# DeltaNet's triangular inverse taken in place in a one-core hybrid layer kernel: the sign moved into the decay products, the negated copy dropped

## The chip, the cores and the metric

The kernel runs on one core of a Trainium2 chip. The metric is the device time of one execution in microseconds. Engines are named as in the profile: PE (TensorE matmul), PEld (its weight load), DVE (VectorE), ACT (ScalarE), POOL (GpSimd), SP (the queue that issues most transfers). On each engine the order of instructions is fixed when the program is built; an instruction whose data are not there holds up all that stand behind it on its engine.

## What is computed

One layer of a hybrid backbone on 128 context and 512 latent tokens, D_MODEL 1024: a token-mixing sub-layer with a gated DeltaNet branch and a short-convolution branch, then a SwiGLU feed-forward part. What the change touches is the DeltaNet's triangular inverse, for 8 heads, 2 directions and chunks of 64 tokens:

```
lower = jnp.where(tri_strict, jnp.einsum('bhncd,bhned->bhnce', kb, k) * decay, 0.0)
tmat = lax.linalg.triangular_solve(eye + lower, jnp.broadcast_to(eye, lower.shape),
                                   left_side=True, lower=True)
u = jnp.einsum('bhnce,bhned->bhncd', tmat, v * beta[..., None])
```

After it a recurrence over the chunks (the scan) makes the outputs and the final state.

## The kernel before, in words

The kernel is written with a tile framework. Instructions are written in program order with priorities; when the program is built, a scheduler orders each engine's instructions by these priorities and by its own estimate of when their data are ready. The order is then fixed. A change in a few instructions of DVE can so move many others, on every engine.

The mixing sub-layer handles the heads in four pairs, 0 to 3. For each pair, `qkv` makes q, k and v by GEMMs, `prepare` makes the chunk matrices, and `scan` runs the recurrence. All GEMMs here are sums of three passes (lines 83, 84, 85), each instruction 128x320; they fill PE in between, in program order at low priority: the GEMMs of `qkv`, `zgate`, `gate_th` and `short`. Of the work around the change:

- `prepare` multiplies the decays `em` and `ea` with the products of k and q from PSUM (L537), copies `em` in quarters into `Md` (L549) and transposes 32x32 blocks on DVE (L553, into `blk`). It negates that into `X` (L554), sets the diagonal to 1 (L555), and takes thirty steps, each of two DVE instructions: `otmp` is a column of `blk` times a row of `X` (L559), and `X` less `otmp` (L561). Two more block transposes give `RT` and `R` (L565, L566).
- PE then makes the off-diagonal blocks: L578 (waits for `RT`), ACT copies `Y` (L583), L589 and L590, and L593 on ACT and L595 on DVE evict them with a factor of -1 into `EW`. L614 and L619/L621 finish `EW`.
- `scan` has eight steps of two halves each: four or eight small matmuls (L643), and then one copy on ACT and one on DVE (L647 or L661) which the next half needs. L673 makes the outputs, L678 to L688 normalise them.
- Interleaved with a pair's inverse, the next pair's `kh` (L448, DVE) is made from a chain of small instructions (L431 to L444), and PE transposes it (L479).
- `row_job` (from the end of pair 3's `prepare` on) adds up modulation rows on DVE, L196, 128x1024 each, from weights of 512 KB.

The tile tag "kb" has one buffer, shared in turn by `kqT`, `blk` and `RT`. The three PSUM buffers of the GEMMs (`d`) are freed by the engine that reads them: for the short convolution these are L716 and L724 on DVE.

Of the kernel before, what the change touches and what calls it, by code (L numbers as in the profile page):

```python
# [9 lines left out]
F32 = mybir.dt.float32  # L10
F32R = mybir.dt.float32r
I32 = mybir.dt.int32
AF = mybir.ActivationFunctionType
ALU = mybir.AluOpType
# [4 lines left out]
P = 128  # L19
# [18 lines left out]
class Kernel:  # L38
# [369 lines left out]
    def prepare(self, p, qkv):  # L408
        nc, dn, dc, g = self.nc, self.da, self.dc, self.g
# [7 lines left out]
        for j in (1, 0, 2):  # L417
            pw = self.psw.tile([P, 1024], F32, name="w", tag="w")
            for t in range(NT):
                nc.tensor.transpose(pw[:, t * P:(t + 1) * P], qkv[j][:, t * P:(t + 1) * P], self.ident)  # L420
            x = dn.tile([P, TOK], F32, name="tk", tag="t25")
            (nc.scalar.copy, nc.scalar.copy, nc.scalar.copy)[j](out=x, in_=pw[:, 0:TOK])
            tok[j] = x
        q, k, v = (tok[j] for j in range(3))
# [31 lines left out]
        for c2 in range(2):  # L456
            s = half(1 - c2)
            for d in range(2):
                nc.gpsimd.tensor_tensor(out=KU[s, d, c2], in1=bc(g["egl"][s, d, :, h2], 64),
                                        in0=self.ident[s, s].unsqueeze(1).unsqueeze(1).broadcast_to([64, NT, 2, 64]),  # L460
                                        op=ALU.mult)
# [14 lines left out]
        for j, x in enumerate((kh, qh)):  # L476
            pw = self.psw.tile([P, 1024], F32, name="w", tag="w")
# [15 lines left out]
        em = dn.tile([P, 2, 2, NT, 64], F32, name="em")  # L493
        ea = dn.tile([P, 2, 2, NT, 64], F32, name="ea")
        for c2 in range(2):
            for t_, d, i in ((em, 0, 0), (em, 1, 2), (ea, 0, 0), (ea, 1, 1)):
                nc.sync.dma_start(out=t_[c2 * 64:c2 * 64 + 64, d].rearrange("p h t x -> p (h t x)"),
                                  in_=g["scr"][i, c2, h2].rearrange("h t x -> (h t x)").unsqueeze(0).broadcast_to([64, TOK]))
# [24 lines left out]
        for ts in (slice(0, 4), slice(4, 5)):  # L523
            m = ts.stop - ts.start
            pw = self.psw.tile([P, 1024], F32, name="w", tag="w")
            for par in range(2):
                for t in range(m):
                    for hd, c2 in ((0, par), (1, 1 - par)):
                        hs = slice(hd * 64, hd * 64 + 64)
                        n = 2 * (ts.start + t) + c2  # L530
                        i = hd * 512 + t * P
                        mm(pw[c2 * 64:c2 * 64 + 64, i:i + P], lhsT=kq3[hs, 0, n, :], rhs=kq3[hs, :, n, :],
                           start=True, stop=True)
            pv = pw.rearrange("p (h t j x) -> p j h t x", h=2, j=2, x=64)[:, :, :, 0:m]
            for e, j in ((em, 0), (ea, 1)):
                for d in range(2):
                    nc.vector.tensor_tensor(out=e[:, d, :, ts], in0=e[:, d, :, ts], in1=pv[:, j], op=ALU.mult)  # L537
        for c2 in range(2):
            nc.gpsimd.dma_start(out=AQ[half(c2), :, c2].rearrange("p d h t x -> p d (h t x)"),
                              in_=ea[half(c2)].rearrange("p d h t x -> p d (h t x)"))  # L540


        Md, EW = self.Md, self.EW
        emv = em.rearrange("p d h t x -> p (d h t) x")
        Ev = [EW[:, :, c2].rearrange("p d h t x -> p d (h t) x") for c2 in range(2)]
        quad = [(c2, b, slice(c2 * 64 + b * 32, c2 * 64 + b * 32 + 32)) for c2 in range(2) for b in range(2)]
        for c2, b, s in quad:
            cp = (nc.vector.tensor_copy, nc.scalar.copy)[b]
            cp(out=Md[s, 0:20], in_=emv[s, :, b * 32:b * 32 + 32])  # L549
        B = dn.tile([P, 32, 32], F32, name="blk", tag="kb")  # L550
        X = dn.tile([P, 32, 32], F32, name="X")
        tmp = dn.tile([P, 256], F32, name="otmp")
        nc.vector.transpose(out=B.rearrange("q r x -> q x r"), in_=Md.rearrange("p m x -> p x m"))  # L553
        nc.vector.tensor_scalar(out=X, in0=B, scalar1=-1.0, scalar2=None, op0=ALU.mult)  # L554
        nc.vector.memset(X.rearrange("q r x -> q (r x)")[:, 0:32 * 32:33], 1.0)  # L555
        for j in range(1, 31):
            n = 31 - j
            t = tmp[:, 0:n * j].rearrange("q (a b) -> q a b", b=j)
            nc.vector.tensor_tensor(out=t, in0=B[:, j + 1:32, j:j + 1].broadcast_to([P, n, j]),  # L559
                                    in1=X[:, j:j + 1, 0:j].broadcast_to([P, n, j]), op=ALU.mult)  # L560
            nc.vector.tensor_tensor(out=X[:, j + 1:32, 0:j], in0=X[:, j + 1:32, 0:j], in1=t, op=ALU.subtract)  # L561

        RT = dn.tile([P, 32, 32], F32, name="RT", tag="kb")
        R = dn.tile([P, 32, 32], F32, name="R")
# [7 lines left out]
        pw = self.psv.tile([P, 1024], F32, name="v", tag="v")  # L572
        Y = dn.tile([P, 20, 32], F32, name="Y")
        for m in range(20):
            for c2 in range(2):
                s0 = slice(c2 * 64, c2 * 64 + 32)
                s1 = slice(c2 * 64 + 32, c2 * 64 + 64)
                mm(pw[s0, m * 32:m * 32 + 32], lhsT=emv[s1, m, 0:32], rhs=RT[s1, m, :], start=True, stop=True,  # L578
                   tile_position=(c2 * 64 + 32, c2 * 64))
        for c2 in range(2):  # L580
            s0 = slice(c2 * 64, c2 * 64 + 32)
            cp = (nc.scalar.copy, nc.scalar.copy)[c2]
            cp(out=Y[s0].rearrange("p m x -> p (m x)"), in_=pw[s0, 0:TOK])  # L583
        pw = self.psv.tile([P, 1024], F32, name="v", tag="v")
# [5 lines left out]
                mm(pw[s1, o], lhsT=Y[s0, 10 + m], rhs=R[s0, 10 + m], start=True, stop=True,  # L590
                   tile_position=(c2 * 64, c2 * 64 + 32))
        for c2, s0, s1 in quads:
            nc.scalar.activation(out=Ev[c2][s0, 0, :, 32:64], in_=pw[s0, 0:320].rearrange("p (m x) -> p m x", x=32),  # L593
                                 func=AF.Copy, scale=-1.0)
            nc.vector.tensor_scalar(out=Ev[c2][s1, 1, :, 0:32], in0=pw[s1, 0:320].rearrange("p (m x) -> p m x", x=32),  # L595
                                    scalar1=-1.0, scalar2=None, op0=ALU.mult)
        return dict(kt=kt, KU=KU, R=RS, AQ=AQ)

    def scan(self, p, pre):
# [139 lines left out]
    def run(self):  # L739
# [422 lines left out]

        def block(ps, A, B, start):
            for k in range(4):
                for n, (x, y) in enumerate(((0, 0), (0, 1), (1, 0))):
                    nc.tensor.matmul(ps, lhsT=A[x][:, k], rhs=B[y][:, k], start=start and k == 0 and n == 0,  # L1166
                                     stop=k == 3 and n == 2, skip_group_check=True)
# [36 lines left out]
        def second(j, v):  # L1204
# [10 lines left out]
            with high():  # L1215
                nc.scalar.copy(out=u2, in_=A)
            B = fd()[:, 0:HALF]
            block(B, o["A12"], B21, True)
# [25 lines left out]
        with tc.manual_schedule(engines={mybir.EngineType.PE}):  # L1244
# [18 lines left out]
            for _ in range(2):  # L1263
                q = quad()
                act += [q[:, i] for i in range(4)]
            prepare(rest[0])
            last = None
            for i, j in enumerate(rest):
                if i + 1 < len(rest):
                    prepare(rest[i + 1], rest[i + 1] < EARLY)  # L1270
                v = first(j)
                if last:
                    third(*last)
                second(j, v)
                last = j, v
# [156 lines left out]
```

## Time and profile before

| | |
|---|---|
| time, median of 3 runs | 1085.77 us (1082.73 to 1088.36) |
| profiled execution: its own time | 1087.67 us |
| profiled execution: its span, first to last instruction | 1085.9 us |
| PE busy | 1021.2 us (94%) |
| DVE busy | 838.9 us (77%) |
| ACT busy | 481.1 us (44%) |

The profiled execution took 1.8 us more than its span, and 1.9 us more than the median of the runs. Pairs 0 to 3 fill the stretch from about 80 us to 460 us of the span; what comes behind are gates, output projections and the feed-forward part.

### The profile page before, as it was taken

Reading aid. Unit: us, or ns where it says so; the run is one execution under the profiler, and the core shown is the slowest. Engines: PE = TensorE matmul, PEld = TensorE weight load, DVE = VectorE, ACT = ScalarE, POOL = GpSimd, SP = SyncE. Lnnn points to the kernel's source line nnn. Section 1 sums busy time; section 2 is a strip of 40 time slices with the busy share of each in tenths; the row PEclk is TensorE's granted clock in tenths of the full one; section 3 lists DMA queues with packets and bytes.
Section 4 is the critical chain, followed back from the end, with each engine's and each line's share of the span. In section 5 each row is a group of like instructions: output and inputs, shape, how many; then the busy total and the mean of one; then the engine's idle time right before and its main releaser. Section 6 shows DMA issues by size and latency. Waiting matters only on the chain.

```text
span 1085.9 us, 19684 instructions
## 1 busy us (share of the span) xinstructions
PE 1021.2 (94%) x7729; PEld 928.0 (85%) x7729; DVE 838.9 (77%) x1702; ACT 481.1 (44%) x923; POOL 142.6 (13%) x168
## 2 busy tenths in 40 slices
PE   6999989988988989999998998999999999999997
PEld 3699988877887888899997888999999999788885
DVE  5767996897898897896896779888787775975336
ACT  5568436415525324425223367444444444623321
POOL 2215421063063060101000000000000000000000
PEclk9999988999999999999999999999999999999999
DMA  9425711254173275555872532323322222552214
GB/s 345 145 91 137 202 54 62 66 127 126 58 174 105 68 165 182 186 180 189 300 234 87 194 126 83 124 96 98 116 79 78 98 78 67 185 172 94 85 39 155
DMA packets 47687, 142.57 MB, mean 131 GB/s; under 512 B 9549, under 2 KB 10066, under 8 KB 47594
## 3 DMA queue, kind: packets, MB, share of 16 engines
q1 hardware_dynamic: 43034, 128.15, 36.2%
q0 software_dynamic: 4560, 13.15, 5.5%
q8 instruction: 61, 1.00, 0.4%
q14 instruction: 32, 0.26, 0.1%
HBM read 118.62 MB, written 12.18 MB: 120 GB/s over the span
## 4 chain that ended last, share of the span: by engine, by line
PE 73%; DVE 16%; ACT 5%; issue 3%; DMA 2%; POOL 1%; SPq 0%; DVEq 0%; ACTq 0%; POOLq 0%
PE acc L1166 19%; PE d L85 8%; PE d L83 8%; PE d L84 8%; PE acc L84 6%; PE acc L83 6%; PE acc L85 6%; PE d L1166 2%; DVE X L561 2%; PE s L643 2%; DVE wl L58 2%; DVE otmp L559 2%; ACT wh L57 1%; PE v L673 1%; PE m L790 1%
## 5 line engine op out<-in xcount | busy, mean ns | idle before, releaser
L83 PE MATMUL d<-hT,wh 128*128 128x320 f32 x720 | 230.0, 320 | 2.0 <-DVE cy L724 2.0
L85 PE MATMUL d<-hT,wl 128*128 128x320 f32 x720 | 230.5, 321 | 0.4 <-DVE wl L58 0.4
L84 PE MATMUL d<-hT,wh 128*128 128x320 f32 x720 | 228.9, 318 | 0.0
L57 ACT CAST wh<-wr 128x512 fp32r<-128x512 f32 x150 | 87.8, 618 | 151.5 <-PE d L84 87.7
L83 PEld LDWEIGHTS d<-hT,wh 128*128 128x128 f32 x720 | 138.9, 193 | 4.6 <-DVE cy L724 2.3
L85 PEld LDWEIGHTS d<-hT,wl 128*128 128x128 f32 x720 | 138.7, 193 | 4.1 <-issue 1.2
L84 PEld LDWEIGHTS d<-hT,wh 128*128 128x128 f32 x720 | 138.8, 193 | 2.2 <-issue 0.5
L58 DVE TENSOR_TENSOR wl<-wr,wh 128x512 fp32r<-128x512 f32 x150 | 102.9, 707 | 40.0 <-ACT wh L57 39.1
L1166 PE MATMUL acc<-mh,wh 128*128 128x320 f32 x288 | 89.6, 311 | 2.0 <-ACT wh L1105 2.0
L1166 PE MATMUL acc<-mh,wl 128*128 128x320 f32 x288 | 89.7, 312 | 0.9 <-DVE wl L1101 0.8
L1166 PE MATMUL acc<-ml,wh 128*128 128x320 f32 x288 | 89.3, 310 | 0.0
L83 PE MATMUL acc<-wh,as 128*128 128x512 f32 x220 | 85.7, 390 | 2.1 <-ACT as L1300 2.1
L84 PE MATMUL acc<-wl,as 128*128 128x512 f32 x220 | 85.6, 389 | 0.0
L85 PE MATMUL acc<-wh,as 128*128 128x512 f32 x220 | 85.5, 389 | 0.0
L196 DVE SCALAR_TENSOR_TENSOR gacc<-wr,cv,gacc 128x1024 f32<-128x1024 f32 x64 | 80.6, 1278 | 4.2 <-DMA wr<-in_w_mod_dram 4.1
L1105 ACT CAST wh<-wr 128x512 fp32r<-128x512 f32 x66 | 40.5, 627 | 72.2 <-PE acc L1166 44.9
L1105 ACT CAST wh<-S 128x512 fp32r<-128x512 f32 x88 | 54.2, 620 | 40.5 <-PE d L1166 17.0
L1101 DVE TENSOR_TENSOR wl<-S,wh 128x512 fp32r<-128x512 f32 x88 | 59.9, 686 | 4.7 <-ACT wh L1105 4.0
L1166 PEld LDWEIGHTS acc<-mh,wh 128*128 128x128 f32 x288 | 54.6, 190 | 2.3 <-ACT wh L1105 2.2
L1166 PEld LDWEIGHTS acc<-mh,wl 128*128 128x128 f32 x288 | 54.5, 189 | 1.4 <-DVE wl L1101 1.4
L1101 DVE TENSOR_TENSOR wl<-wr,wh 128x512 fp32r<-128x512 f32 x66 | 44.8, 688 | 13.9 <-ACT wh L1105 13.2
L1166 PEld LDWEIGHTS acc<-ml,wh 128*128 128x128 f32 x288 | 54.5, 189 | 0.0
(365 smaller groups left out, 2326.2 us busy)
## 6 DMA issues: line engine op xcount, KB each, us to landing
wr<-in_w_ffn_in_dram SPq DMA_DIRECT2D x50, 512.0 KB
wr<-in_w_in_dram SPq DMA_DIRECT2D x45, 512.0 KB
wr<-in_w_mod_dram SPq DMA_DIRECT2D x32, 512.0 KB
wr<-in_w_ffn_out_dram SPq DMA_DIRECT2D x22, 512.0 KB
mr<-in_w_mod_dram SPq DMA_DIRECT2D x16, 512.0 KB
thd<-gt SPq DMA_DIRECT2D x16, 320.0 KB
bth<-thd SPq DMA_DIRECT2D x16, 320.0 KB
wr<-in_w_br_dram SPq DMA_DIRECT2D x8, 512.0 KB
```

The lines of the kernel that those rows point to most:

```text
L57: (high or nc.scalar.copy)(out=hi[:, s], in_=raw[:, s])
L58: (low or nc.vector).tensor_tensor(out=lo[:, s], in0=raw[:, s], in1=hi[:, s].bitcast(F32), op=ALU.subtract)
L83: mm(out, lhsT=ah, rhs=bh, start=start, stop=False)
L84: mm(out, lhsT=ah, rhs=bl, start=False, stop=False)
L85: mm(out, lhsT=al, rhs=bh, start=False, stop=stop)
L196: nc.vector.scalar_tensor_tensor(out=acc[v], in0=w, scalar=self.cv[:, k, v:v + 1], in1=acc[v], op0=ALU.mult, op1=ALU.add)
L559: nc.vector.tensor_tensor(out=t, in0=B[:, j + 1:32, j:j + 1].broadcast_to([P, n, j]), in1=X[:, j:j + 1, 0:j].broadcast_to([P, n, j]), op=A ...
L561: nc.vector.tensor_tensor(out=X[:, j + 1:32, 0:j], in0=X[:, j + 1:32, 0:j], in1=t, op=ALU.subtract)
L643: mm(ps[half(c2), o:o + 64], lhsT=w(d, c2, t, hd), rhs=R[:, d, c2, t, hd, :], start=True, stop=True)
L1101: tt = lambda o, a, b, op: nc.vector.tensor_tensor(out=o, in0=a, in1=b, op=op)
L1105: nc.scalar.copy(out=dst[0], in_=src)
L1166: nc.tensor.matmul(ps, lhsT=A[x][:, k], rhs=B[y][:, k], start=start and k == 0 and n == 0, stop=k == 3 and n == 2, skip_group_check=True)
```

## The change

The product with the decays takes the sign: the two multiplications of `em` become scalar_tensor_tensor with -1, those of `ea` with +1. `em` is negated from there on, so the transposed blocks are what L554 made before: L553 writes `X` itself, L554 and the tile `blk` go, the steps read their column from `X`, and add where they subtracted. The off-diagonal products have the sign in `em` already, so the two evictions copy.

```diff
-            for e, j in ((em, 0), (ea, 1)):
+            for e, j, sign in ((em, 0, -1.0), (ea, 1, 1.0)):
                 for d in range(2):
-                    nc.vector.tensor_tensor(out=e[:, d, :, ts], in0=e[:, d, :, ts], in1=pv[:, j], op=ALU.mult)
+                    nc.vector.scalar_tensor_tensor(out=e[:, d, :, ts], in0=e[:, d, :, ts], scalar=sign, in1=pv[:, j],
+                                                   op0=ALU.mult, op1=ALU.mult)
...
-        B = dn.tile([P, 32, 32], F32, name="blk", tag="kb")
         X = dn.tile([P, 32, 32], F32, name="X")
         tmp = dn.tile([P, 256], F32, name="otmp")
-        nc.vector.transpose(out=B.rearrange("q r x -> q x r"), in_=Md.rearrange("p m x -> p x m"))
-        nc.vector.tensor_scalar(out=X, in0=B, scalar1=-1.0, scalar2=None, op0=ALU.mult)
+        nc.vector.transpose(out=X.rearrange("q r x -> q x r"), in_=Md.rearrange("p m x -> p x m"))
...
-            nc.vector.tensor_tensor(out=t, in0=B[:, j + 1:32, j:j + 1].broadcast_to([P, n, j]),
+            nc.vector.tensor_tensor(out=t, in0=X[:, j + 1:32, j:j + 1].broadcast_to([P, n, j]),
                                     in1=X[:, j:j + 1, 0:j].broadcast_to([P, n, j]), op=ALU.mult)
-            nc.vector.tensor_tensor(out=X[:, j + 1:32, 0:j], in0=X[:, j + 1:32, 0:j], in1=t, op=ALU.subtract)
+            nc.vector.tensor_tensor(out=X[:, j + 1:32, 0:j], in0=X[:, j + 1:32, 0:j], in1=t, op=ALU.add)
...
-            nc.scalar.activation(out=Ev[c2][s0, 0, :, 32:64], in_=pw[s0, 0:320].rearrange("p (m x) -> p m x", x=32),
-                                 func=AF.Copy, scale=-1.0)
-            nc.vector.tensor_scalar(out=Ev[c2][s1, 1, :, 0:32], in0=pw[s1, 0:320].rearrange("p (m x) -> p m x", x=32),
-                                    scalar1=-1.0, scalar2=None, op0=ALU.mult)
+            nc.scalar.copy(out=Ev[c2][s0, 0, :, 32:64], in_=pw[s0, 0:320].rearrange("p (m x) -> p m x", x=32))
+            nc.vector.tensor_copy(out=Ev[c2][s1, 1, :, 0:32], in_=pw[s1, 0:320].rearrange("p (m x) -> p m x", x=32))
```

The order that the scheduler makes changes with it on PE, DVE, ACT and SP; POOL's does not. Three places follow. Lines of the changed kernel stand one or two away from those before: the steps' L559 and L561 are L560 and L562, and behind L595 all are one less (the scan's L643 is L642, its copies L647 and L661 are L646 and L660, L673 is L672).

On DVE, at the start of pair 0's inverse, before:

```order
L549 COPY Md<-em 32x640 x2
L553 STREAM_TRANSPOSE blk<-Md 128x32x32
L554 TENSOR_SCALAR X<-blk 128x1024
L555 MEMSET X 128x32
L559 TENSOR_TENSOR otmp<-blk,X 128x30
L561 TENSOR_TENSOR X<-X,otmp 128x30
L559 TENSOR_TENSOR otmp<-blk,X 128x58
L561 TENSOR_TENSOR X<-X,otmp 128x29x2
L559 TENSOR_TENSOR otmp<-blk,X 128x84
L58 TENSOR_TENSOR wl<-wr,wh 128x512 x2
```

and there of the changed kernel:

```order
L551 COPY Md<-em 32x640 x2
L554 STREAM_TRANSPOSE X<-Md 128x32x32
L555 MEMSET X 128x32
L560 TENSOR_TENSOR otmp<-X 128x30
L562 TENSOR_TENSOR X<-X,otmp 128x30
L560 TENSOR_TENSOR otmp<-X 128x58
L562 TENSOR_TENSOR X<-X,otmp 128x29x2
L560 TENSOR_TENSOR otmp<-X 128x84
L562 TENSOR_TENSOR X<-X,otmp 128x28x3
L560 TENSOR_TENSOR otmp<-X 128x108
L562 TENSOR_TENSOR X<-X,otmp 128x27x4
L58 TENSOR_TENSOR wl<-wr,wh 128x512 x2
```

The negated copy is gone, and the weight split `wl` (L58, for a GEMM) stands three instructions of the inverse further back.

On PE, in the second half of pair 3's scan, before (L83 to L85 are GEMM passes):

```order
L643 MATMUL s<-RS,EW 64x64 x4
L85 MATMUL d<-hT_75,wl 128x320
L83 MATMUL d<-hT_75,wh 128x320
L84 MATMUL d<-hT_76,wh 128x320
L673 MATMUL v<-RS,AQ 64x64
...
L643 MATMUL s<-RS,KU 64x64 x4
L84 MATMUL d<-hT_76,wh 128x320
```

and there of the changed kernel:

```order
L642 MATMUL s<-RS,EW 64x64 x4
L672 MATMUL v<-RS,AQ 64x64
L642 MATMUL s<-RS,KU 64x64 x4
L642 MATMUL s<-RS,EW 64x64 x4
L672 MATMUL v<-RS,AQ 64x64
L642 MATMUL s<-RS,KU 64x64 x4
...
L672 MATMUL v<-RS,AQ 64x64 x16
L642 MATMUL s<-RS,EW 64x64 x4
L208 MATMUL m<-cph,onesr 1x512 x2
```

Before, GEMM passes stand between the halves of the scan's steps; in the changed kernel none stand there in this part. Counted over the whole order of PE, 1604 GEMM passes stood ahead of the first L614 of pair 3 and 1577 do now; between the L643 group whose GEMM count was 1679 (now 1656) and the last L673 group of the scan stood 89, and stand none now.

On DVE, in the same part of the scan, before:

```order
L661 COPY RS<-s 64x128
L196 SCALAR_TENSOR_TENSOR gacc<-wr,cv,gacc 128x1024
L647 COPY RS<-s 64x128
L196 SCALAR_TENSOR_TENSOR gacc<-wr,cv,gacc 128x1024
L58 TENSOR_TENSOR wl<-wr,wh 128x512
L661 COPY RS<-s 64x128
L58 TENSOR_TENSOR wl<-wr,wh 128x512
L196 SCALAR_TENSOR_TENSOR gacc<-wr,cv,gacc 128x1024
L647 COPY RS<-s 64x128
```

and there of the changed kernel, down to the scan's last copy:

```order
L660 COPY RS<-s 64x128
L196 SCALAR_TENSOR_TENSOR gacc<-wr,cv,gacc 128x1024
L646 COPY RS<-s 64x128
L58 TENSOR_TENSOR cpl<-gacc,cph 128x512 x2
L660 COPY RS<-s 64x128
L716 TENSOR_SCALAR cy<-cx,tapsc 128x640
L379 SCALAR_TENSOR_TENSOR cy<-cx,tapsc,cy 128x10x63
L646 COPY RS<-s 64x128
L58 TENSOR_TENSOR cpl<-gacc,cph 128x512 x2
```

Nine scan copies in a row (L646 and L660 in turn) have one L196 between each two and no `wl` any more; what follows them are the rows shown, with `cy` of the short convolution, which stood ahead of the scan before.

## Rows read from the trace of the kernel before

**Rows 1.** The page: busy us of each engine, share of the span, instructions.

```profile
PE 1021.2 (94%) x7729; PEld 928.0 (85%) x7729; DVE 838.9 (77%) x1702; ACT 481.1 (44%) x923; POOL 142.6 (13%) x168
```

**Rows 2.** Stretches: length, then busy us of PE, PEld, DVE, ACT, POOL, clock.

```profile
100.00:150.00 50.00, 42.42 (x297) 40.50 (x296) 47.71 (x113) 21.84 (x35) 23.33 (x23) 0.93 0.51 138
300.00:350.00 50.00, 43.13 (x496) 41.17 (x498) 47.07 (x108) 19.11 (x36) 27.26 (x30) 0.93 0.59 150
418.90:437.90 19.00, 19.00 (x233) 17.11 (x234) 16.63 (x23) 5.57 (x13) 0.00 (x0) 1.00 0.47 149
437.90:459.10 21.20, 21.20 (x209) 17.29 (x209) 17.29 (x27) 8.84 (x23) 1.22 (x2) 1.00 0.66 216
```

**Rows 3.** PE's timeline: start, us, instruction, idle before and its releaser.

```profile
140.79 1.30 PE L479 MATMUL w<-ident,kh 128*128 128x128 f32 x5 [5.40 <-DVE kh L448]
222.31 0.48 PE L479 MATMUL w<-ident,kh 128*128 128x128 f32 x1 [2.62 <-DVE kh L448]
243.10 0.41 PE L83 MATMUL d<-hT,wh 128*128 128x320 f32 x1 [2.00 <-DVE cy L724]
249.54 1.55 PE L578 MATMUL v<-RT,em 32*32 32x32 f32 x80 [1.92 <-DVE RT L565]
324.91 0.76 PE L479 MATMUL w<-ident,kh 128*128 128x128 f32 x5 [2.06 <-DVE kh L448]
335.84 1.54 PE L578 MATMUL v<-RT,em 32*32 32x32 f32 x80 [2.26 <-DVE RT L565]
```

**Rows 4.** Line 554: duration ns minimum, median, maximum.

```profile
L554 DVE TENSOR_SCALAR X<-blk x4: 674/680/695, 121.0 to 369.2; 128x1024 f32<-128x1024 f32 x4
```

**Rows 5.** DVE's timeline: tensor_tensor and scalar_tensor_tensor, one PSUM input each.

```profile
232.96 0.81 DVE L683 TENSOR_TENSOR ob<-ro,v 128x640 f32<-128x640 f32 x1
234.69 0.89 DVE L688 SCALAR_TENSOR_TENSOR zf<-v,onorm,zf 128x640 f32<-128x640 f32 x1
```

**Rows 6.** DVE's timeline around 400 us and 414 us.

```profile
404.47 0.69 DVE L58 TENSOR_TENSOR wl<-wr,wh 128x512 fp32r<-128x512 f32 x1
408.14 0.47 DVE L716 TENSOR_TENSOR cx<-cx,d 128x320 f32<-128x320 f32 x1
416.24 0.55 DVE L717 TENSOR_SCALAR cy<-cx,tapsc 128x640 f32<-128x640 f32 x1
417.33 0.88 DVE L379 SCALAR_TENSOR_TENSOR cy<-cx,tapsc,cy 128x630 f32<-128x630 f32 x1
```

**Rows 7.** DVE's timeline late in pair 3's scan.

```profile
438.24 0.29 DVE L647 COPY RS<-s 64x128 f32<-64x128 f32 x1
...
451.34 0.28 DVE L647 COPY RS<-s 64x128 f32<-64x128 f32 x1
451.55 1.27 DVE L196 SCALAR_TENSOR_TENSOR gacc<-wr,cv,gacc 128x1024 f32<-128x1024 f32 x1
452.92 0.28 DVE L661 COPY RS<-s 64x128 f32<-64x128 f32 x1
...
454.90 1.29 DVE L58 TENSOR_TENSOR cpl<-gacc,cph 128x512 fp32r<-128x512 f32 x2
...
458.41 0.28 DVE L647 COPY RS<-s 64x128 f32<-64x128 f32 x1
```

**Rows 8.** PE's timeline: GEMM passes at full clock.

```profile
128.19 0.31 PE L83 MATMUL d<-hT,wh 128*128 128x320 f32 x1
128.33 0.31 PE L84 MATMUL d<-hT,wh 128*128 128x320 f32 x1
```

**Rows 9.** Stretches around two idle spells of PE, columns as in rows 2.

```profile
130.00:140.00 10.00, 5.39 (x37) 5.12 (x35) 10.00 (x23) 3.57 (x5) 6.72 (x7) 1.00 0.27 90
140.00:150.00 10.00, 9.21 (x45) 9.24 (x46) 9.03 (x17) 1.99 (x4) 3.45 (x2) 0.66 0.25 88
240.00:250.00 10.00, 6.08 (x60) 5.59 (x60) 9.69 (x24) 2.60 (x6) 0.00 (x0) 1.00 0.58 149
250.00:260.00 10.00, 8.61 (x225) 7.79 (x219) 6.20 (x11) 6.67 (x14) 1.20 (x1) 1.00 0.62 188
```

## The prediction

> **What bounds the kernel now.** The page comes first: PE is busy 94% of the span, DVE 77% [rows 1]. So PE's total work is the floor, and the time moves only with the stretches in which PE waits or runs at a lower clock. The table of stretches shows where: between 100 and 150 us PE is busy 42.42 of 50 us while DVE is busy 47.71; between 300 and 350 it is 43.13 against 47.07 [rows 2]. There DVE is the engine that the others wait for. In pair 3's scan it is the other way round: from 418.9 to 459.1 us PE is busy all the time and DVE four fifths of it [rows 2]. PE's timeline then names the waits in the pairs' stretch: PE, which works in order, stands at the transposes of `kh` for 5.40, 2.62 and 2.06 us, at L578 for `RT` 1.92 and 2.26 us, once at a GEMM for `cy` 2.00 us [rows 3]. All are DVE results that come out among the inverse's instructions. They are what a shorter inverse could win. The covered scan is what a new order could lose.
>
> **Part 1, the copy that goes.** L554 takes 0.68 us, four times [rows 4]: 2.7 us of DVE work. It stands in a chain with no other work of its own (transpose, negate, steps), so nothing hides it from `RT`. The memset and the 240 step instructions keep their counts and shapes; adding in place of subtracting, and reading the column from `X`, change neither the number of inputs nor their place in SBUF, so I take them at nothing. No step waits for a new thing: column j of `X` is last written before step j in both versions. The tag "kb" loses a user: L553 need not wait for `kqT` any more, which it never did in the end.
>
> **Part 2, the sign.** 32 multiplications become scalar_tensor_tensor: 16 of 512 columns, 16 of 128, one input from PSUM. The nearest rows are 0.81 us for a tensor_tensor and 0.89 us for a scalar_tensor_tensor, both of 640 columns with a PSUM input [rows 5]. In proportion that is 0.06 us for 512 and 0.02 us for 128, in sum 1.3 us; the bounds are 0 and 32 times 0.08, or 2.6 us. I take 1.3, since the row differs in having its factor in memory and not as a constant, and nothing says which way that goes. The two evictions become copies of the same size; I take them at nothing, bounded by the 0.08 us by which the two instructions differ [rows 5], for each of 16, either way; they lie beside GEMMs on PE. So the direct saving on DVE is 2.7 - 1.3 = 1.4 us, worth 0.1% if all of it reached the end.
>
> **Part 3, the new order ahead of pair 3's scan.** Counting DVE's order between the block transpose L553 and `RT`, each pair loses the 0.68 us copy, and some work moves past `RT`: for pair 0 an L381 with half the columns of the 0.88 us L379 [rows 6], some 0.5 us, for pairs 1 and 2 a scan copy of 0.29 us [rows 7] and an L716 of 0.47 us [rows 6], for pair 3 two `wl` of 0.69 us [rows 6]. That makes about 1.2, 1.0, 1.3 and 2.0 us, 5.5 in sum; less 1.3 for part 2 the chain of inverses comes 4.2 us earlier to pair 3's scan. PE's order answers to it: at its first L614 of pair 3 PE has done 1577 GEMM passes and not 1604. A pass starts every 0.14 to 0.15 us (128.19, 128.33) [rows 8], so 27 passes are 4.0 us of PE work put off till later. 4.2 us earlier with 4.0 us less done is a gain of 0.2 us; I take 0. The bounds: if the moved work only comes back behind `RT`, the chain is 1.4 us earlier and the loss is 2.6 us; if all waits of rows 3 other than the first went, the gain is 2.62 + 2.00 + 1.92 + 2.06 + 2.26 = 10.9 us. I leave the first out because `kh` of pair 1 still stands behind one more step of the inverse, three instructions of 0.4 us, less the copy.
>
> GpSimd shortens what I trust of those waits. The Trainium skill ("SBUF — State Buffer", section "Who interferes with whom") says that a DVE instruction with two SBUF inputs and a GpSimd instruction that reads SBUF lock each other out. By it the inverse's steps keep being caught, as their inputs all stay in SBUF, and the change moves such stalls but removes none; the sum would stand.
>
> **Part 4, pair 3's scan uncovered.** This is the term that decides. Before, 89 GEMM passes stand between the halves of its last steps, and PE is busy for all of the 21.20 us [rows 2]; 89 times 0.147 is 13.1 us, so L643, L673, L208 and L209 have the other 8.1. In the changed order none of the 89 is there. PE must wait after each group of L643 for the copy, and on DVE a 1.27 us L196 stands between each two copies: 451.34 to 452.92 is 1.58 us a half [rows 7]. The nine copies in a row take eight times 1.58 = 12.6 us; then come the `cpl` pair of 1.29 us and a copy of 0.29 [rows 7], and `cy` with 0.55 and 0.88 us [rows 6] and the last copy: 3.3 us. That is 15.9 us between the copies which before lie at 438.24 and 458.41 [rows 7], 20.2 us. So the scan ends 4.3 us sooner, with 13.1 us of GEMMs not done. They come back later, in the stretch from 460 us on where PE has no slack: a loss of 13.1 - 4.3 = 8.8 us. The lower bound is a cadence without L196's full length, say 1.28 us a half, as if a copy could hide: 2.4 us less, 6.4. The upper bound is the old pace: 13.1.
>
> What is queued behind: L673's last group, then the GEMMs. On DVE the short convolution's `cy` (L717 on) now comes at the scan's end, so the second `cy` product and SP's store of it are late by some 20 us, with SP's next weight loads behind that store. Three weights are loaded ahead of the store, though: the GEMM count stands at 1656, and loads up to pass 1824 are ahead of it, 24.7 us of work. I take 0.
>
> **Part 5, the clock.** After 4.6 us of idle in the slice 130 to 140 the granted clock was 0.66 in the next [rows 9]; after 3.9 us in the slice 240 to 250 it stayed 1.00 [rows 9]. At the lower of the two levels, 1.2 GHz and not 2.4, a slice at 0.66 ran 6.8 us at half pace, up to 3.4 us lost. The uncovered scan leaves PE idle for about 15.9 - 8.1 = 7.8 us in short gaps. I take 1.5 us, between 0 and 3.4. The Trainium skill ("TensorE: Matmul & The Clock Gate", section "What's actually happening") says that the default is the throttled clock and activity releases it. By that the clock would fall here, and the term would be the 3.4 rather than 1.5; rows 9 show one spell that did and one that did not.
>
> **The sum.** 0 + 8.8 + 1.5 = 10.3 us against the profiled execution's own 1087.67: 1098.0. That execution lies 1.9 us above the median of the runs, 1085.77; on the median's scale the forecast is 1096 us, slower by 0.9%. Its own range is 1091.5 to 1102.
>
> **The rivals.**
>
> *The waits ahead win it back (not slower).* If the shorter chain empties the five waits of part 3, 10.9 us, that pays for parts 4 and 5: 1085.77 - 10.9 + 10.3 = 1085. For it: pair 2's `kh` stands in PE's new order behind 22 small L673 groups and 26 passes, some 5 us later than now, and pair 3's behind 22 passes more. Against it: `kh` also stands later on DVE, behind the normalisation's first instructions, and waits for DVE add up to a DVE that has hardly got less to do. It decides from about 5 us of vanished waits.
>
> *The order matters little (the change does only what the diff says).* Then 1.4 us are left: 1084. It needs the uncovered halves to be covered by something that I don't see in PE's order. If the scan is not what holds PE there and part 3 goes well too, faster by over 0.5% is possible, 1078 to 1080.
>
> *The put-off GEMMs meet late weights.* If the loads behind the late store of `cy`, or the splits `wl` behind L196s, come too late, PE waits again after the scan. A wait like that at `cy`, 2.00 us [rows 3], two or three times, makes 1100 to 1104.
>
> **Chances.** The forecast 0.56, the waits won back 0.22, little effect 0.12, late weights 0.10. What a measurement of this kernel can tell from no change is about 0.5%, 5.4 us: 1080.3 to 1091.2. From the forecast 0.06 falls inside it, from the second 0.19 (0.03 below), from the third 0.07 (0.05 below). So slower 0.60, same 0.32, faster 0.08. To leave out no more than 2 in 10 the range goes from 1083, just under the little effect and with most of the waits won back, to 1102, the forecast's upper end.
>
> **What would show it.** In the profile after: DVE without L554, L537 as scalar_tensor_tensor of 0.6 to 0.75 us at 512 columns; in pair 3's scan PE idle for 7 to 9 us in ten gaps, each ended by a scan copy, the copies 1.5 to 1.7 us apart with an L196 between; the clock below 1.00 in that slice or the next; from there to the end the same PE work as now, some 9 us later. I would be wrong if PE's waits ahead of the scan fall by more than 5 us, if pair 3's scan starts much more than 4 us earlier, or if the halves run faster than DVE's order lets me think.

## The result, and the profile after

The changed kernel takes 1095.28 us (median of 6 runs, 1090.06 to 1097.92), the kernel before 1085.63 us (6 runs beside it): a ratio of 1.0084 with a 95% interval of 1.0064 to 1.0104. It is slower, by 0.64 to 1.04%; forecast were 1096 us. The profiled executions have spans of 1094.2 and 1085.9 us. Ratios here and below stand as recorded with the runs; they can differ by up to 0.001 from the quotient of the medians, which is 1.0089 here. One execution of e1 (3419.57 us) and one of before beside it (1970.42 us) lie far outside all others and are left out of the medians and ratios below.

The page's line of busy times, which answers to [rows 1], and the stretches that answer to [rows 2] (length, busy us of PE, PEld, DVE, ACT, POOL, clock, DMA share, GB/s). The changed kernel's pair 3 scan, counted from the first L613 before it, runs from 408.4 to 445.0 us; its uncovered part begins at 427.7.

```profile
PE 1023.7 (94%) x7729; PEld 930.4 (85%) x7729; DVE 836.0 (76%) x1698; ACT 480.4 (44%) x923; POOL 142.3 (13%) x168
```

```profile
100.00:150.00 50.00, 42.34 (x301) 40.41 (x301) 48.19 (x118) 23.12 (x36) 22.75 (x23) 0.93 0.51 136
300.00:350.00 50.00, 40.27 (x481) 38.40 (x480) 45.54 (x104) 19.38 (x33) 20.53 (x22) 0.93 0.57 146
408.40:427.70 19.30, 18.94 (x234) 16.95 (x233) 15.95 (x20) 5.47 (x12) 0.00 (x0) 1.00 0.49 164
427.70:445.00 17.30, 9.87 (x122) 6.50 (x121) 16.20 (x24) 5.93 (x16) 1.47 (x2) 0.69 0.55 183
430.00:440.00 10.00, 5.75 (x86) 4.72 (x84) 9.81 (x13) 2.70 (x8) 0.00 (x0) 0.54 0.59 193
440.00:450.00 10.00, 8.18 (x88) 5.52 (x85) 8.26 (x17) 4.76 (x11) 3.29 (x4) 0.78 0.21 57
```

DVE has four instructions and 2.9 us of work less: the four copies, and nothing added for the sign. What matters is the fourth stretch. Before, PE was busy for all of the scan [rows 2]; now it idles 17.30 - 9.87 = 7.43 us there, and the clock's mean is 0.69.

PE's timeline in the scan (start, us, instruction, idle before it and what ended that) shows the gaps:

```profile
429.70 0.45 PE L642 MATMUL s<-RS,EW 128*64 128x64 f32 x8 [1.19 <-DVE RS L660]
431.33 0.70 PE L642 MATMUL s<-RS,KU 128*64 128x64 f32 x8 [0.49 <-DVE RS L646]
432.73 0.69 PE L642 MATMUL s<-RS,EW 128*64 128x64 f32 x8 [0.70 <-DVE RS L660]
434.24 0.70 PE L642 MATMUL s<-RS,KU 128*64 128x64 f32 x8 [0.82 <-DVE RS L646]
...
445.00 2.62 PE L672 MATMUL v<-RS,AQ 128*64 128x64 f32 x44 [1.26 <-DVE RS L646]
```

And DVE's timeline there, which answers to [rows 7]:

```profile
427.71 0.29 DVE L646 COPY RS<-s 64x128 f32<-64x128 f32 x1
...
435.54 0.29 DVE L660 COPY RS<-s 64x128 f32<-64x128 f32 x1
435.86 1.28 DVE L196 SCALAR_TENSOR_TENSOR gacc<-wr,cv,gacc 128x1024 f32<-128x1024 f32 x1
437.18 0.28 DVE L646 COPY RS<-s 64x128 f32<-64x128 f32 x1
437.39 1.27 DVE L196 SCALAR_TENSOR_TENSOR gacc<-wr,cv,gacc 128x1024 f32<-128x1024 f32 x1
438.58 0.28 DVE L660 COPY RS<-s 64x128 f32<-64x128 f32 x1
...
444.66 0.28 DVE L646 COPY RS<-s 64x128 f32<-64x128 f32 x1
```

Up to 438.58 us each copy that PE waits for stands behind an L196, on a DVE that works without a pause; the last three stand behind an L196 and 0.64 us of idle, the `cpl` pair, and `cy`. From 427.71 to 438.58 there are seven intervals, 1.55 us each in the mean; from the first copy to the last it takes 16.95 us.

The waits ahead of the scan, which answer to [rows 3], on PE's timeline:

```profile
142.83 1.30 PE L479 MATMUL w<-ident,kh 128*128 128x128 f32 x5 [5.48 <-DVE kh L448]
...
218.11 1.09 PE L672 MATMUL v<-RS,AQ 128*64 128x64 f32 x30 [3.40 <-DVE RS L646]
...
247.02 1.20 PE L579 MATMUL v<-RT,em 32*32 32x32 f32 x35 [2.47 <-DVE RT L566]
...
308.42 0.73 PE L686 MATMUL v<-ident,ob 128*128 128x128 f32 x5 [2.10 <-DVE ob L682]
320.66 0.52 PE L479 MATMUL w<-ident,kh 128*128 128x128 f32 x3 [2.26 <-DVE kh L448]
330.67 0.50 PE L579 MATMUL v<-RT,em 32*32 32x32 f32 x15 [2.60 <-DVE RT L566]
```

The 2.62 us wait for pair 2's `kh` is gone; waits for `RS` at 218 us and for `ob` at 308 us stand there in its place, and those for `RT` are no shorter. All of PE's waits from 80 to 400 us together are 33.5 us before, 32.5 in e1 (the order of before, see below) and 32.5 in the changed kernel: on the whole the shorter inverse emptied none of them.

### The profile page after: what moved, and what is told of

Read it like the earlier page. It is cut to its first block, busy times and chain, and to the rows that moved or that the text cites. A ratio compares the mean times of both kernels' runs of the same rounds, so it can differ in the third digit from the quotient of the medians.

```text
span 1094.2 us, 19680 instructions
## 1 busy us (share of the span) xinstructions
PE 1023.7 (94%) x7729; PEld 930.4 (85%) x7729; DVE 836.0 (76%) x1698; ACT 480.4 (44%) x923; POOL 142.3 (13%) x168
## 4 chain that ended last, share of the span: by engine, by line
PE 72%; DVE 17%; ACT 4%; issue 3%; DMA 3%; POOL 1%; SPq 0%; DVEq 0%; ACTq 0%; POOLq 0%
PE acc L1165 20%; PE d L85 8%; PE d L84 8%; PE d L83 7%; PE acc L84 6%; PE acc L83 6%; PE acc L85 6%; PE d L1165 3%; PE s L642 2%; DVE X L562 2%; DVE wl L58 2%; DVE otmp L560 2%; DVE gacc L196 1%; PE v L672 1%; PE m L789 1%
## 5 line engine op out<-in xcount | busy, mean ns | idle before, releaser
L85 PE MATMUL d<-hT,wl 128*128 128x320 f32 x720 | 229.9, 320 | 0.4 <-DVE wl L58 0.4
L83 PE MATMUL d<-hT,wh 128*128 128x320 f32 x720 | 228.4, 318 | 1.2 <-DVE cy L723 1.2
L85 PEld LDWEIGHTS d<-hT,wl 128*128 128x128 f32 x720 | 138.7, 193 | 3.2 <-issue 0.9
L83 PEld LDWEIGHTS d<-hT,wh 128*128 128x128 f32 x720 | 138.7, 193 | 3.1 <-DVE cy L723 1.4
L58 DVE TENSOR_TENSOR wl<-wr,wh 128x512 fp32r<-128x512 f32 x150 | 104.0, 717 | 39.3 <-ACT wh L57 38.8
L196 DVE SCALAR_TENSOR_TENSOR gacc<-wr,cv,gacc 128x1024 f32<-128x1024 f32 x64 | 80.4, 1278 | 12.6 <-DMA wr<-in_w_mod_dram 12.4
L83 PE MATMUL acc<-wh,as 128*128 128x512 f32 x220 | 86.5, 393 | 2.1 <-ACT as L1299 2.1
L85 PE MATMUL acc<-wh,as 128*128 128x512 f32 x220 | 85.7, 390 | 0.0
```

Of the source, the lines that this page charges most:

```text
L58: (low or nc.vector).tensor_tensor(out=lo[:, s], in0=raw[:, s], in1=hi[:, s].bitcast(F32), op=ALU.subtract)
L83: mm(out, lhsT=ah, rhs=bh, start=start, stop=False)
L85: mm(out, lhsT=al, rhs=bh, start=False, stop=stop)
L196: nc.vector.scalar_tensor_tensor(out=acc[v], in0=w, scalar=self.cv[:, k, v:v + 1], in1=acc[v], op0=ALU.mult, op1=ALU.add)
```

## The experiments

The theory: the arithmetic of the change is worth its 2.7 us of DVE work; the loss comes from the scheduler's new order, in which pair 3's scan stands without GEMM passes between its halves, and from the lower clock in and behind it. Rivals: the new instructions themselves cost the time; the late `cy` of the short convolution and the transfers behind it cost it; the clock costs nothing by itself. Medians below are of runs on one chip in each batch; before took 1085.89 us beside the first four, 1085.81 us beside the others.

**The changed arithmetic in the old order** (e1). A multiplication of `X` by one stands where the negation stood, and with it every engine's order is that of before.

```diff
+        nc.vector.tensor_scalar(out=X, in0=X, scalar1=1.0, scalar2=None, op0=ALU.mult)
```

> The whole change in arithmetic (sign with the decays, inverse in place, plain evictions), but with one more DVE instruction where the negated copy stood: X times 1.0 onto itself. With it the order on PE, POOL and SP is word for word that of before, and on DVE and ACT only kinds of instructions differ. Theory A (the new order costs the time, the arithmetic does not): 1085.6 us within 2, ratio to before 0.998 to 1.002. Rival B (in-place steps and the three-operand products are dearer on the chip than they look): 1090 or more, as the changed kernel.

Measured: 1085.55 us, ratio 1.000 (0.9984 to 1.0015). So scalar_tensor_tensor, the addition, the column from `X` and the copying evictions cost nothing together that can be told, within some 1.7 us. The products' line at 512 columns is closer, and says the same of the first alone (busy us, mean ns of one, idle before), in the changed kernel and before:

```profile
L538 DVE SCALAR_TENSOR_TENSOR em<-em,w 128x512 f32<-128x512 f32 x8 | 5.2, 681 | 3.0 <-ACT em L517 2.1 <-PE w L532 0.9
```

```profile
L537 DVE TENSOR_TENSOR em<-em,w 128x512 f32<-128x512 f32 x8 | 5.2, 681 | 8.0 <-ACT em L517 5.5 <-PE w L532 2.4
```

What is left is the order.

**The cover restored from outside** (e2, and e3 with the same edit in the kernel before). One `gate_th` and one step of the row job are written ahead of the second short convolution instead of behind it:

```diff
-        self.short(1, hT)
-        steps(2)
         self.gate_th(5, hT)
         steps(1)
+        self.short(1, hT)
+        steps(2)
```

> The changed kernel, with one more gate GEMM (number 5) written ahead of the second short convolution, and the modulation steps with it. The order is the changed kernel's up to pair 2's inverse; in pair 3's scan GEMM passes stand between the halves again. Theory A: the covered scan gives back 8 us or more and the gain ahead of it, about 5 us in the trace, stays: 1079 to 1084, PE without waits in pair 3's scan. Rival C (the loss lies in lower clock and waits behind the scan, whatever its cover): 1091 or more.

> The kernel before with the same GEMM written ahead of the second short convolution: what the move does without the change. Pair 3's scan is covered here as it was. Theory A: 1083 to 1088, so that the change alone, with cover in both, is worth 3 to 6 us. Rival B: the changed kernel of this order is not faster than this one.

Measured: in the changed kernel 1081.42 us, ratio 0.9965 (0.9948 to 0.9983); in the kernel before 1085.36 us, ratio 0.9992 (0.9975 to 1.0009). The edit is worth some 13 to 14 us where the scan was uncovered (1095.28 - 1081.42 = 13.9 by medians of two batches, 12.9 by the ratios) and nothing that can be told where it was covered. PE's order has GEMM passes between all halves again (1767 passes stand ahead of the scan's last L642 group, not 1656), and the stretches of e2 show PE full at full clock where the changed kernel had 5.75 us at 0.54:

```profile
430.00:440.00 10.00, 10.00 (x89) 8.00 (x87) 8.37 (x12) 2.53 (x8) 0.00 (x0) 1.00 0.66 202
440.00:450.00 10.00, 10.00 (x122) 8.87 (x122) 9.40 (x13) 4.44 (x12) 0.00 (x0) 1.00 0.72 236
```

Up to pair 2's inverse e2's order is the changed kernel's. The waits there are of the same sort and size: between 80 and 470 us 10.1 us for `kh` and 6.0 for `RS` at L672, in the changed kernel 9.0 and 5.8. So those waits are no part of the loss. And with the scan covered in both, the change is worth 0.9965 / 0.9992 = 0.9973, or 2.9 us (3.9 by the medians); the intervals of the two, added as squares, leave it between 0.03 and 0.5%.

**The short convolution's `cy` made urgent** (e4: both products; e5: the second alone, the one that had slid to the scan's end).

```diff
-        nc.vector.tensor_scalar(out=y, in0=cx, scalar1=self.tapsc[:, 1, i:i + 1], scalar2=None, op0=ALU.mult)
-        self.conv(cx, self.tapsc, i, y, 0, 10, True)
+        with (self.urgent() if i == 1 else nullcontext()):
+            nc.vector.tensor_scalar(out=y, in0=cx, scalar1=self.tapsc[:, 1, i:i + 1], scalar2=None, op0=ALU.mult)
+            self.conv(cx, self.tapsc, i, y, 0, 10, True)
```

(This is e5; e4 has `self.urgent()` for both.)

> The changed kernel, with the short convolution's own products on DVE (the line of cy and the four behind it) at high priority. Pair 3's scan has GEMM passes between its halves, but 1730 ahead of its last group where before had 1762. Theory A: 1079 to 1085. Rival C: 1091 or more.

> The changed kernel with only the second cy product (the one that had slid to the end of pair 3's scan, and with it SP's store and the weight loads behind that store) made urgent, so that it comes in time again. Pair 3's scan stays uncovered: 1680 GEMM passes stand ahead of its late groups and none between them. Theory (the uncovered scan is the loss, the late cy and the late store cost nothing): as the changed kernel, 1091 to 1097 us, ratio to before 1.005 to 1.010; the scan's copies 1.4 to 1.65 us apart. Rival (the late cy and the loads behind its store are the loss): 1082 to 1087 us, ratio 0.997 to 1.001, with the scan as uncovered as before.

Measured: e4 1084.88 us, ratio 0.9994 (0.9979 to 1.001); e5 1096.24 us, ratio 1.0088 (1.0065 to 1.011). In e4 the new order happens to cover the scan (1730 passes), and the loss is gone; the gain that e2 has is not there, and why is open. In e5 `cy` comes in time (L717 at 409.15 us, ahead of the scan's uncovered part) and the scan stays uncovered (1680 passes throughout), and the loss is all there. On the ledger of the next section its scan alone loses 6.6 us beside e1 (44.38 us with 119 passes, for 50.01 with 202). That speaks for the scan and against the late `cy`, but e5 is not clean: it has a new wait of its own later on PE's timeline, which the changed kernel has not:

```profile
527.74 0.42 PE L83 MATMUL d<-yah,wh 128*128 128x320 f32 x1 [2.23 <-DVE bth L987]
530.02 0.39 PE L83 MATMUL d<-ybh,wh 128*128 128x320 f32 x1 [0.26 <-DVE bth L987]
549.72 0.42 PE L83 MATMUL d<-yah,wh 128*128 128x320 f32 x1 [1.86 <-DVE bth L987]
```

On DVE an L196 ahead of the first `bth` waited 4.53 us for its weights. Less PE's 4.3 us (2.23, 0.26 and 1.86) e5 would stand at 1092, still 6 us above before; so the late `cy` can carry two fifths of the loss at most (4.3 of 10.4), if e5's new wait is counted for it, and none if not.

**Spare matmuls in the scan** (e6: two a half, e7: four). They keep PE busy while it waits, with products that nobody reads; the scan's own work is not changed. The trace has two records for each of these products, as for each of L642.

```diff
+            if p == 3 and s_ >= 2:
+                for _ in range(2):
+                    mm(ps[:, 128:256], lhsT=self.ident, rhs=self.ident, start=True, stop=True)
```

> The changed kernel with two spare 128x128 products of the identity after each half of pair 3's scan from step 2 on, written into PSUM columns that nobody reads: extra work whose result is unused, which only keeps PE busier while it waits for the scan's copies. No GEMM pass comes into the scan by it (1656 throughout). Theory that the clock has a part of the loss of its own (2 to 3 us): granted clock higher in 430 to 450 us, time 1091 to 1094, ratio to the changed kernel 0.997 to 0.999. Rival (all of the loss is the GEMM passes put off, the clock costs nothing): no change, 1094 to 1097, whatever the clock shows. If the spare products delay the scan's own: over 1097.

> The same with four spare products a half, some 0.9 us of PE work and so about all of PE's idle time in a half; the order takes a few GEMM passes (from 1658 to 1687) back into the scan with it. Clock theory: granted clock 1.00 from 430 to 460 us, 1089 to 1093 us, of which up to 4 are passes that come back into the scan. Rival (clock costs nothing): what the passes in the scan give alone, 1091 to 1096. If the spare products hold up the scan: the copies more than 1.7 us apart and over 1096.

Measured: e6 1097.24 us, ratio 1.0106 (1.0086 to 1.0127); e7 1106.03 us, ratio 1.0178 (1.0149 to 1.0207). By the total, neither gained; the stretches tell why. In e6:

```profile
430.00:440.00 10.00, 6.74 (x74) 5.11 (x75) 8.63 (x12) 1.45 (x6) 0.00 (x0) 1.00 0.61 207
440.00:450.00 10.00, 8.74 (x118) 5.99 (x119) 9.24 (x17) 4.53 (x11) 2.71 (x3) 1.00 0.35 108
```

The clock stayed at 1.00, in this one execution. From the scan's last L672 group (L678 in e6) to the first wide column sum (L208, 512 columns into `d`) stand the same 888 GEMM passes as in the changed kernel, and they took 134.60 us (449.21 to 583.81) and not 137.32 (445.00 to 582.32). Of these 2.7 us the clock has about 1.2: the changed kernel's last group, shown above, took 2.62 us; in e6 and in before the same 44 matmuls took 1.50:

```profile
449.21 1.50 PE L678 MATMUL v<-RS,AQ 128*64 128x64 f32 x44
```

```profile
459.03 1.50 PE L673 MATMUL v<-RS,AQ 128*64 128x64 f32 x44
```

and the changed kernel's clock is back at 1.00 from 447.9 us on:

```profile
430.80:441.00 10.20, 6.31 (x83) 4.76 (x82) 9.35 (x14) 2.70 (x8) 0.00 (x0) 0.50 0.52 165
445.00:447.90 2.90, 2.90 (x45) 2.51 (x46) 2.46 (x5) 0.24 (x1) 1.70 (x2) 0.50 0.03 7
447.90:450.00 2.10, 2.10 (x15) 1.90 (x14) 1.60 (x4) 1.54 (x4) 0.12 (x1) 1.00 0.18 4
```

The rest is not the clock's: 0.7 us are three column sums into `m` (L208, L209) that e6 has elsewhere, and 0.7 us are GEMM passes that come a little farther apart at full clock. But the spare products stood in the scan's own way. They write the tile `s` that the copies read, so ACT's copy starts when the last of them has ended (436.97 us, behind 436.22 and 0.71). DVE's waits for ACT's, and the copies come 1.76 us apart:

```profile
436.22 0.71 PE L646 MATMUL s<-ident 128*128 128x128 f32 x4
```

```profile
435.50 0.28 DVE L666 COPY RS<-s 64x128 f32<-64x128 f32 x1 [0.29 <-ACT RS L666]
435.70 1.27 DVE L196 SCALAR_TENSOR_TENSOR gacc<-wr,cv,gacc 128x1024 f32<-128x1024 f32 x1
437.26 0.29 DVE L649 COPY RS<-s 64x128 f32<-64x128 f32 x1 [0.28 <-ACT RS L649]
```

From `RT` of pair 3 to the last group that made 47.94 us for 45.76, so 2.2 us were lost again, and another 2.0 us ahead of `RT` in this execution, over the same passes. In e7 the clock fell all the same (0.73 in 430 to 440 us), so these two do not show that spare work keeps it up. The scheduler answered to the longer halves with two L196 between copies, which came 2.84 us apart:

```profile
432.14 0.29 DVE L666 COPY RS<-s 64x128 f32<-64x128 f32 x1
432.47 2.48 DVE L196 SCALAR_TENSOR_TENSOR gacc<-wr,cv,gacc 128x1024 f32<-128x1024 f32 x2
434.98 0.28 DVE L649 COPY RS<-s 64x128 f32<-64x128 f32 x1
```

Both miss as ways to win time. They show what sets the pace: DVE's work between two copies, and what stands ahead of the copy on PE.

**More gates ahead** (e8). Three `gate_th` ahead of the second short convolution, in the changed kernel:

```diff
         self.gate_th(3, hT)
-        steps(2)
-        self.short(1, hT)
-        steps(2)
         self.gate_th(5, hT)
-        steps(1)
         self.gate_th(6, hT)
+        steps(3)
+        self.short(1, hT)
+        steps(2)
```

> The changed kernel with three gate_th products written ahead of the second short convolution in pair 3's part, and the inverse's steps between them; the same work, another order. GEMM passes ahead of the scan's last group are 1762 of before's 1768, so the scan is covered. Theory (the change is worth its direct saving once the scan is covered): 1080 to 1083 us, ratio to before 0.995 to 0.998, like the milder move of one gate_th. Rival (the milder move was luck of its own order): 1085 or more. If the gates ahead of the short convolution starve its chain: a new PE wait for cy or cx, over 1088.

Measured: 1082.45 us, ratio 0.9969 (0.9954 to 0.9983). A third order that covers the scan, and as fast as e2. Both are faster than either kernel. What e8's edit does in the kernel before was not run, so its gain is not the change's alone.

## Why the prediction came out as it did

The loss had the place, the mechanism and nearly the size that were forecast. The ledger sets landmarks on PE against each other; a GEMM pass not yet done counts 0.147 us, from the forecast's [rows 8]. e1 stands beside before as a second execution of the same order.

| stretch | before, us (passes) | e1, us | changed, us (passes) | loss against before / e1 |
|---|---|---|---|---|
| start to pair 3's L578 | 408.54 (1566) | 404.56 | 399.24 (1539) | -5.3 / -1.3 |
| to the scan's last L673 group | 50.49 (202) | 50.01 | 45.76 (117) | 7.8 / 8.2 |
| to the first wide L208 | 118.22 (776) | 118.22 | 137.32 (888) | 2.6 / 2.6 |
| to the end of the span | 508.65 | 508.21 | 511.88 | 3.2 / 3.7 |
| sum | | | | 8.3 / 13.2 |

The sums are the differences of the spans, 1094.2 less 1085.9 and 1081.0; by the medians it is 9.7. That this lies so near the 10.3 forecast is partly luck: 1.3 us of part 2 that were not spent and a gain of 1.3 to 5.3 us ahead of the scan stand against 3.2 to 3.7 us at the end, none of them forecast.

- **Part 1** held: 2.7 us of DVE work went. e2 over e3 gives 2.9 us at the end, where the scan is covered; that agrees, but the interval (0.03 to 0.5%, or 0.3 to 5.4 us) is too wide to tell it from twice as much.
- **Part 2** was mis-sized, within its bounds: 1.3 us forecast, 0 measured (681 ns each at 512 columns). The row with a factor from memory was no guide to one with a constant.
- **Part 3**: forecast 0, measured a gain of 1.3 us beside e1 and 5.3 beside before's own profile. The same order differs by 4 us between these two executions at that point (the clock's mean up to there is 0.97 in e1 and 0.96 in before), so it can't be told closer. Pair 3's scan did start 6.0 (e1) or 10.4 us (before) earlier and not 4.2, which the forecast had named as a sign against it; 27 passes less were done by then, as forecast.
- **Part 4** held: 8.8 us forecast, 7.8 to 8.2 measured, on the ledger's somewhat longer stretch; 7.43 us of idle where 7 to 9 were forecast; 16.95 us between the copies and not 15.9, at 1.55 us a half and not 1.58, because one copy came 0.64 us late, behind an L672 group on PE and ACT's half, and the first `cy` product, 0.55 us before [rows 6], took 1.05.
- **Part 5** held: 1.5 us forecast. The ledger shows 2.6 us behind the scan, but only 1.2 of them are the clock (the last L672 group and a column sum behind it, at 0.50); 0.3 are one column sum more and 1.1 GEMM passes that took more than the ledger's 0.147 us each. Within the scan the lower clock cost at most the 0.64 us of the late copy: L642 took 0.70 us in place of 0.45, but beside an L196, and the copies came 1.64 us apart before the clock fell at 430.8 us and 1.40 to 1.65 after. So it is 1.2 to 1.9 us in all, and the 1.5 were well sized. By the rule of the Trainium skill that the forecast weighed ("TensorE: Matmul & The Clock Gate", section "What's actually happening") the clock would fall here, and the trace agrees: it was 0.50, the lower level of 1.2 GHz, from 430.8 to 441.0 us. The 3.4 us that the forecast set beside that rule did not come, since PE was waiting for DVE anyway in most of that time.
- The last row was not forecast. About half of it is a longer spell at the lower clock at 580 to 600 us (0.89 and 0.77 in the two slices, for 0.83 and 1.00 before), half one at 930 us; the last section comes back to the second. Neither follows from a step of the change that a run here shows.
- **The rivals.** The waits won back: one went, 2.62 us, and others took its place (3.40 and 2.10 us), and the waits' sum is that of e1, 32.5 us. That fits the case against it, "a DVE that has hardly got less to do"; no run tests that reason by itself. The order matters little: excluded by e1 and e2. Late weights: the changed kernel has no such wait behind the scan; e5 has one of that sort, 4.3 us at `bth`, so the risk was real and was not met. The stalls of DVE beside GpSimd that the forecast mentions were tested by no run.

## What to carry to other kernels

With a static scheduler, taking out an instruction can move work that has nothing to do with it. Compare the two orders, find the stretch in which small dependent steps were covered by independent work, and count what is left between them. If the cover is gone, move a piece of independent work in the program text: here two calls written two lines earlier turned +0.84% into -0.35%.

## What the runs showed that was not expected

The same wait of PE, for `as` behind 2.11 us of idle near 926 to 933 us, ended at full clock in one execution and at a lower one in another. The changed kernel's slice, and that of before:

```profile
930.00:940.00 10.00, 7.89 (x30) 6.24 (x29) 9.23 (x14) 9.03 (x15) 1.84 (x2) 0.83 0.68 234
```

```profile
920.00:930.00 10.00, 7.89 (x42) 6.64 (x43) 7.43 (x13) 6.32 (x11) 1.84 (x2) 1.00 0.83 288
```

Both have 7.89 us of busy PE; the clocks are 0.83 and 1.00. On PE's timeline the nine passes behind the wait took 3.64 us (932.78 to 936.42) and 2.27 us (925.86 to 928.13), so a fall costs 1.4 us here:

```profile
932.78 0.80 PE L83 MATMUL acc<-wh,as 128*128 128x512 f32 x1 [2.11 <-ACT as L1299]
936.42 0.40 PE L83 MATMUL acc<-wh,as 128*128 128x512 f32 x1
```

```profile
925.86 0.50 PE L83 MATMUL acc<-wh,as 128*128 128x512 f32 x1 [2.11 <-ACT as L1300]
928.13 0.40 PE L83 MATMUL acc<-wh,as 128*128 128x512 f32 x1
```

All ten traces have this wait of 2.11 us. The clock stayed at 1.00 in three (before, e1, and e6, which met it at 934.98 us) and fell in seven, the changed kernel and e3 (at 921.19 us) among them. So the length of the wait doesn't settle it; that it is chance, and not each kernel's own order, is likely but not shown at this place, with one trace of each. Chance there is: executions of before, beside the first four experiments, go from 1082.13 us at a mean clock of 0.984 to 1090.01 us at 0.976. In the scan, too, PE's busy share doesn't settle it: with 5.75 us of busy PE in 430 to 440 us the clock was 0.54, with 5.20 in e5 it was 0.75, with 7.08 in e7 0.73, with 6.74 in e6 1.00. The Trainium skill ("TensorE: Matmul & The Clock Gate", section "What's actually happening") says that the gate's watching runs on freely and is not reset when a kernel starts; by that the same spell would be met now one way, now the other, as here, but no run here tests it.

A scalar_tensor_tensor with a constant and one input from PSUM takes as long as the tensor_tensor it replaces: 681 ns each, in the mean of eight at 512 columns.
